# A hybrid decoder block on one core: a start-up branch taken out, a wider mask product, and a row finish moved into the next pass

## The chip, the core and the metric

One core of a Trainium2 chip runs one program, which holds the whole decoder block. TensorE (PE in the rows) multiplies; its weight loads (PEld) have rows of their own. VectorE (DVE), ScalarE (ACT) and GpSimd (POOL) work beside it, and SyncE (SP) mostly issues DMAs; ACT and POOL can issue DMAs too. Each engine works through its own list of instructions in order and waits on semaphores for the others. The metric is the device time of one execution in microseconds. Runs of a kernel spread by a few tenths of a per cent.

## What is computed

One layer over 1024 rows of width 1024, cut to what matters here:

```python
hn = rmsnorm(h, norm_mix_g);  proj = hn @ w_in            # split into the parts of both attentions and two gates
o_a = indexed_sparse_attention(a_q, a_k, a_v, i_q, i_k, i_w, positions, topk=256)
o_b = latent_attention(q_nope, q_rope, k_nope, k_rope, v_b, positions)
h = h + (sigmoid(g_a) * (o_a @ w_branch_a) + sigmoid(g_b) * (o_b @ w_branch_b)) @ w_out
u = causal_depthwise_conv(rmsnorm(h, norm_ffn_g) @ w_up);  gate, val = split(u)
h = h + (silu(gate) * val) @ w_down                       # 2816 -> 1024
return rmsnorm(h, norm_final_g)
```

Both attentions mask by position: a key counts where its position is not above that of the query. `setup_inputs` gives the positions 0 to 1023, so that the mask is the plain causal one; a kernel has to be right for any positions.

## The kernel before

**Arithmetic.** Every float32 operand is split into a rounded high part (`split`, line 150, on ACT for the most part) and the rest (line 156, a subtraction on DVE or POOL), and `mm3` (lines 180 to 182) multiplies high by high, high by low and low by high. All 128x512 products are of this kind.

**Two versions in one program.** `Block(..., True)` is written for rising positions and uses the triangle; `Block(..., False)` takes any. `emit` (line 1880 on) first loads the positions on SP and ACT, compares neighbours on DVE (lines 1902 to 1907), sums the flags over the partitions with a small PE product (line 1908), writes a flag (line 1909), and every engine loads it into a register and branches (`tc.If(rising > 0)`). The first block then runs; when it finds a choice of keys too close to call, it writes `redo` (line 837, DVE). At the end every engine loads `redo`, and branches over the second block.

**The start of the block.** `load_x` (line 530 on) sets a tile to zero, multiplies it 12 times to warm PE (line 233), and loads the first weights (line 486) and rows of x (line 544) on SP; DVE and POOL split the weights (lines 152 and 156), ACT and DVE scale and split x (lines 549 and 550). `prologue` builds constants (lines 451 to 464), the triangle `tri` and an identity in bfloat16 among them.

**The mask product.** `scores` (line 695 on) adds the triangle on PE: between the products of a diagonal tile (line 711) stands one product of the identity with `tri` (line 710), 128x128 in bfloat16, whose neighbours are float32 products of 256 to 512 columns. There are 80 in an execution.

**The end.** `ffn_down` goes through seven passes (`plan`, p = 0 to 6) of K = 11 steps, four row blocks (qb) to a step; three matmuls each make 132 in a pass. A step needs two operands, s and t: both are formed from loaded rows by subtractions on POOL (lines 1778 to 1785 in `down_prepare`) and then split, high part on ACT, low part on DVE. The loads of `down_fetch` (line 1724) go by SP and take tiles of one ring (`AS` of them), which the squares and scaled rows use as well. After the last step of a pass the results are added to the rows `H` on DVE (line 1799, `add`). Row blocks 0 to 3 are complete after p = 5, blocks 4 to 7 after p = 6. A complete block is squared and summed on ACT (line 1815), scaled by the gain on POOL (line 1821), and `finish` works out the reciprocal root on DVE: the two half sums are added (line 1827), and `rsqrt` (lines 163 to 174) makes three Newton steps of two small operations each. ACT (line 1834) or DVE (line 1836) then multiplies, and SP stores (line 1837). A scheduler sets the order on each engine when the program is built: it is static, and code that is written later tends to stand later.

## Time and profile before

| | us |
|---|---|
| median of three runs (lowest, highest) | 1614.48 (1614.17, 1618.14) |
| the profiled execution, own time | 1617.39 |
| its span in the trace | 1615.5 |
| PE busy | 1514.8 |
| DVE busy | 1210.2 |
| POOL busy | 918.4 |
| ACT busy | 783.0 |

PE is busy for 94% of the span. The places where it isn't are few, and two of them lie at the ends: ahead of the first product, and in and behind the last pass. A row of the timeline has the start, the duration, the engine and line, the operation with its operands, and in brackets how long the engine was idle before it and on whom it waited. A matmul's duration is longer than the distance to the next one, since they are pipelined; it is the distance of starts that counts.

### The profile page before, as it was taken

How to read it: one execution, taken by the hardware profiler on the slowest of the kernel's cores; microseconds unless marked ns; L12 is line 12 of the kernel's file. 1: busy time of each engine (PE TensorE's matmuls, PEld its weight loads, DVE VectorE, ACT ScalarE, POOL GpSimd, SP SyncE). 2: the span in 40 equal slices, each digit the busy share in tenths (PEclk: the TensorE clock that was granted, in tenths of full speed). 3: DMA queues.
4: the chain of work that ended last, by engine and by line, in shares of the span. 5: the costliest groups of instructions: out<-in, count | busy, mean ns of one | idle time of the engine just before them, and what ended most of it. 6: DMA issues, size and time to landing. Idle time of an engine off the chain costs nothing. (4 is left out here: it accounts for less than half of the span.)

```text
span 1615.5 us, 21528 instructions
## 1 busy us (share of the span) xinstructions
PE 1514.8 (94%) x7312; PEld 1248.7 (77%) x7312; DVE 1210.2 (75%) x1959; ACT 783.0 (48%) x1437; POOL 918.4 (57%) x758
## 2 busy tenths in 40 slices
PE   8979999989899999999999788999999999989985
PEld 7768888877677777898878677888888887768864
DVE  7268999934578887885635986878877776895996
ACT  3635522223367787775422544444444544434434
POOL 3141222511666767665622689888877773586773
PEclk9989999989999999999999899999999999999997
DMA  6321132420200023213752122222222205854333
GB/s 220 133 95 60 53 102 97 131 92 32 100 14 17 14 82 95 72 60 123 238 193 79 46 79 79 79 78 79 88 82 90 93 26 207 312 178 134 127 99 138
DMA packets 74841, 166.23 MB, mean 103 GB/s; under 512 B 9634, under 2 KB 14114, under 8 KB 74722
## 3 DMA queue, kind: packets, MB, share of 16 engines
q1 hardware_dynamic: 64496, 142.74, 26.7%
q10 hardware_dynamic: 7634, 13.64, 2.3%
q0 software_dynamic: 2592, 8.39, 1.3%
q8 instruction: 59, 0.97, 0.2%
q14 instruction: 60, 0.49, 0.1%
HBM read 123.94 MB, written 40.53 MB: 102 GB/s over the span
## 5 line engine op out<-in xcount | busy, mean ns | idle before, releaser
L182 PE MATMUL tc<-tc,tc 128*128 128x512 f32 (+2 forms) x1420 | 546.0, 385 | 7.5 <-POOL tc L156 5.6
L180 PE MATMUL tc<-tc,tc 128*128 128x512 f32 (+2 forms) x1420 | 542.3, 385 | 8.1 <-ACT tc L598 2.4
L181 PE MATMUL tc<-tc,tc 128*128 128x512 f32 (+2 forms) x1420 | 546.7, 385 | 1.2 <-POOL tc L156 1.0
L156 POOL TENSOR_TENSOR tc<-tc,tc 128x512 fp32r<-128x512 f32 (+2 forms) x182 | 300.8, 1659 | 246.0 <-ACT tc L150 229.4
L150 ACT ACTIVATE tc<-tc 128x512 fp32r<-128x512 f32 (+1 forms) x362 | 230.3, 659 | 350.0 <-PE tc L181 219.9
L180 PEld LDWEIGHTS tc<-tc,tc 128*128 128x128 f32 x1420 | 271.2, 191 | 63.8 <-ACT tc L598 2.8
L182 PEld LDWEIGHTS tc<-tc,tc 128*128 128x128 f32 x1420 | 271.2, 191 | 60.2 <-POOL tc L156 6.2
L181 PEld LDWEIGHTS tc<-tc,tc 128*128 128x128 f32 x1420 | 270.4, 190 | 54.0 <-POOL tc L156 1.3
L156 DVE TENSOR_TENSOR tc<-tc,tc 128x512 fp32r<-128x512 f32 x184 | 223.1, 1245 | 45.4 <-ACT tc L150 38.8
L181 PE MATMUL tc<-tc 128*128 128x512 f32 x332 | 133.5, 405 | 12.0 <-DVE tc L156 11.8
L1142 POOL TENSOR_SCALAR tc<-tc,tc 128x128 f32<-128x128 f32 (+7 forms) x128 | 95.1, 748 | 69.3 <-DVE tc L1141 55.8
L182 PE MATMUL tc<-tc 128*128 128x512 f32 x332 | 131.7, 400 | 0.4 <-DVE tc L156 0.4
L180 PE MATMUL tc<-tc 128*128 128x512 f32 x332 | 124.2, 399 | 3.8 <-ACT tc L150 3.5
L1140 ACT ACTIVATE tc<-tc,tc 128x128 f32<-128x128 f32 (+7 forms) x128 | 96.4, 753 | 33.0 <-DVE tc L1134 15.7
L1674 DVE SCALAR_TENSOR_TENSOR tc<-tc,tc,tc 128x1023 f32<-128x1023 f32 x44 | 65.1, 1482 | 53.7 <-ACT tc L1673 53.6
L711 PE MATMUL tc<-tc 128*128 128x384 f32 (+4 forms) x352 | 90.0, 370 | 8.4 <-DVE tc L644 5.7
L1675 DVE SCALAR_TENSOR_TENSOR tc<-tc,tc,tc 128x1022 f32<-128x1022 f32 x44 | 93.6, 2126 | 1.4
L181 PEld LDWEIGHTS tc<-tc 128*128 128x128 f32 x332 | 63.9, 192 | 31.2 <-DVE tc L156 18.6
L711 PE MATMUL tc<-tc,tc 128*128 128x512 f32 (+4 forms) x288 | 78.0, 386 | 8.6 <-ACT tc L1140 7.9
L180 PEld LDWEIGHTS tc<-tc 128*128 128x128 f32 x332 | 63.3, 192 | 18.9 <-ACT tc L150 5.4
L711 PEld LDWEIGHTS tc<-tc 128*128 128x128 f32 x352 | 61.5, 194 | 18.0 <-DVE tc L644 6.5
L182 PEld LDWEIGHTS tc<-tc 128*128 128x128 f32 x332 | 64.0, 193 | 14.6 <-DVE tc L156 1.5
(260 smaller groups left out, 2466.6 us busy)
## 6 DMA issues: line engine op xcount, KB each, us to landing
tc<-tc SPq DMA_DIRECT2D x144, 256.0 KB, 3.3
tc<-in_w_up SPq DMA_DIRECT2D x44, 512.0 KB, 3.7
tc<-in_w_down SPq DMA_DIRECT2D x77, 256.0 KB, 4.3
tc<-tc ACTq DMA_DIRECT2D x52, 256.0 KB, 2.0
tc<-tc SPq DMA_DIRECT2D x20, 512.0 KB, 2.6
tc<-in_w_g SPq DMA_DIRECT2D x16, 512.0 KB, 3.7
tc<-tc POOLq DMA_DIRECT2D x24, 256.0 KB, 2.4
tc<-in_w_c SPq DMA_DIRECT2D x10, 512.0 KB, 4.1
```

Source lines behind the costliest of these rows:

```text
L150: self.last_split = nc.scalar.activation(hi, src, AF.Copy)
L156: e.tensor_tensor(lo, src, hi.bitcast(F32), op=OP.subtract)
L180: x = [mm(ps, lhs[0], rhs[0], start=start, stop=False, **kw), mm(ps, lhs[0], rhs[1], start=False, stop=False, **kw), mm(ps, lhs[1], rhs[0] ...
L181: mm(ps, lhs[0], rhs[1], start=False, stop=False, **kw),
L182: mm(ps, lhs[1], rhs[0], start=False, stop=stop, **kw)]
L711: self.last_score = mm(ps[:, j * 512:j * 512 + n], l, r[:, o:o + n], start=i == 0, stop=i == len(lhs) - 1)
L1140: self.last_exp = nc.scalar.activation(p3, src, AF.Exp, bias=nm, scale=-1.0, accum_out=l)
L1142: nc.gpsimd.tensor_scalar(p, p, l, 0.0, op0=OP.mult, op1=OP.add)
L1674: v.scalar_tensor_tensor(o[:, 1:], x[:, :S - 1], cw[:, t, 1:2], o[:, 1:], op0=OP.mult, op1=OP.add)
L1675: v.scalar_tensor_tensor(o[:, 2:], x[:, :S - 2], cw[:, t, 0:1], o[:, 2:], op0=OP.mult, op1=OP.add)
```

## The change

The flag and its branch at the start are gone: the first block always runs. The comparison of neighbouring positions is kept, as `rising` at the end of `prologue`, on six small DVE operations with two loads on the ACT queue; it counts into `bad`, so that positions that don't rise set `redo`, and the second block then runs as before.

The mask product takes the type of its neighbours and is 256 columns wide: `tri` is a triangle between two blocks of zeros, of which the needed 256 columns are cut out, and the identity is a copy of the same type.

The row finish is written anew. `partial` works out the half that is known early (POOL, after p = 1 and p = 4). `finish` takes a square root on ACT, a reciprocal on DVE and one Newton step, four DVE operations instead of eleven, and its stores go on the ACT queue where ACT multiplied. For blocks 0 to 3, the adds, squares, scaling and finish are no longer written at the end of p = 5: `close` is called after the steps k = 1 to 4 of p = 6, a block a step.

```diff
-            self.tri = self.t(c, [P, P], BF16)
-            v.tensor_scalar(self.tri, jp, 0.0, BIG, op0=OP.is_gt, op1=OP.mult)
-            self.ident_b = self.t(c, [P, P], BF16)
-            v.tensor_copy(self.ident_b, self.ident)
+            self.tri = self.t(c, [P, 3 * P], F32R)
+            v.tensor_scalar(self.tri[:, :P], jp, 0.0, None, op0=OP.mult)
+            v.tensor_scalar(self.tri[:, P:2 * P], jp, 0.0, BIG, op0=OP.is_gt, op1=OP.mult)
+            v.tensor_scalar(self.tri[:, 2 * P:], jp, 0.0, None, op0=OP.mult)
+            self.ident_r = self.t(c, [P, P], F32R)
+            v.tensor_copy(self.ident_r, self.ident)
...
+            self.rising()
...
-                    e = j * 512 + (n if W == cw else W)
-                    mm(ps[:, e - P:e], self.ident_b, self.tri, start=False, stop=False, skip_group_check=True)
+                    e = j * 512 + n
+                    mm(ps[:, e - 256:e], self.ident_r, self.tri[:, P if W < cw else 0:][:, :256], start=False, stop=False,
+                       skip_group_check=True)
...
+    def rising(self):
+        nc, v = self.nc, self.nc.vector
+        pr = self.a["pos_r"]
+        pi, kh, kl = [self.kd[:, o:o + 9].bitcast(I32) for o in (768, 784, 800)]
+        d1, d2 = [self.kd[:, o:o + 8] for o in (816, 832)]
+        nc.scalar.dma_start(pi[:P - 1], bass.AP(tensor=pr.tensor, offset=pr.offset, ap=[[8, P - 1], [1, 9]]))
+        nc.scalar.dma_start(pi[P - 1:], pr[:, S - 9:])
...
+        v.tensor_scalar(d1, d1, 0.0, 0.0, op0=OP.is_le, op1=OP.add, accum_out=self.bad[:, 0:1])
...
+        def partial(b):
+            e = int(b >= 4)
+            x = self.t(dn, [P, 2], F32, tag="ss4", bufs=8)
+            g.tensor_scalar(x[:, 0:1], squares[b][:, e:e + 1], 1.0 / D, EPS, op0=OP.mult, op1=OP.add)
+            g.tensor_scalar(x[:, 1:2], x[:, 0:1], -0.5, 0.0, op0=OP.mult, op1=OP.add)
+            known[b] = x
         def finish(b):
-            v.tensor_add(ss, s2[:, 0:1], s2[:, 1:2])
-            v.tensor_scalar(ss, ss, 1.0 / D, EPS, op0=OP.mult, op1=OP.add)
-            self.rsqrt(c, r, ss, 1)
+            e = int(b < 4)
+            s, x = squares[b][:, e:e + 1], known[b]
+            r, t, y = [self.t(dn, [P, 1], F32, tag=k, bufs=3) for k in ("r3", "t3", "y3")]
+            nc.scalar.activation(r, s, AF.Sqrt, scale=1.0 / D, bias=x[:, 0:1])
+            v.scalar_tensor_tensor(t, s, -0.5 / D, x[:, 1:2], op0=OP.mult, op1=OP.add)
+            v.reciprocal(r, r)
+            v.scalar_tensor_tensor(t, r, t, r, op0=OP.mult, op1=OP.mult)
+            v.scalar_tensor_tensor(y, t, 1.5, r, op0=OP.add, op1=OP.mult)
             for hf in (1, 0):
...
-                nc.sync.dma_start(self.out[b * P:(b + 1) * P, cs], x)
+                (nc.scalar if by_act else nc.sync).dma_start(self.out[b * P:(b + 1) * P, cs], x)
...
+                if late and k >= LATE:
+                    close(*late.pop(0))
             for qb in range(4):
...
                 for rh, hf in plan[p][2]:
+                    if p == 5:
+                        late.append((p, rh, hf, qb))
+                    else:
+                        close(p, rh, hf, qb)
...
-    with tc.If(rising > 0):
-        Block(tc, a, out, True, {"redo": redo}).run()
+    Block(tc, a, out, True, {"redo": redo}).run()
```

`close` holds what stood in the loop before (add, square, scale, finish, and `partial` where the early half is squared).

**On DVE, where p = 5 goes over into p = 6.** Before, the two low pieces of step k = 4 (rows 1737 and 1741; L156, line 156) stand between the Newton operations (lines 163 to 174) of four blocks:

```order
1730 L1827 TENSOR_TENSOR tc_13915<-tc_12875 128x1
1731 L170 SCALAR_TENSOR_TENSOR tc_13839<-tc_13835,tc_13842 128x1
1732 L1828 TENSOR_SCALAR tc_13888<-tc_13888 128x1
1733 L170 SCALAR_TENSOR_TENSOR tc_13866<-tc_13862,tc_13869 128x1
1734 L1828 TENSOR_SCALAR tc_13915<-tc_13915 128x1
1735 L174 SCALAR_TENSOR_TENSOR tc_13835<-tc_13839,tc_13835 128x1
1736 L163 TENSOR_SCALAR tc_13892<-tc_13888 128x1
1737 L156 TENSOR_TENSOR tc_3245<-tc_12267,tc_3245 128x512
1738 L174 SCALAR_TENSOR_TENSOR tc_13862<-tc_13866,tc_13862 128x1
1739 L163 TENSOR_SCALAR tc_13919<-tc_13915 128x1
1740 L170 SCALAR_TENSOR_TENSOR tc_13839<-tc_13835,tc_13842 128x1
1741 L156 TENSOR_TENSOR tc_3245<-tc_13808,tc_3245 128x512
```

Now, in the same place, with the lines of the changed kernel (157 is the old 156; 1859 to 1862 are the new `finish`; rows 1717 and 1719 are step k = 3, rows 1724 and 1727 step k = 4):

```order
1717 L157 TENSOR_TENSOR tc_3210<-tc_12231,tc_3210 128x512
1718 L1859 SCALAR_TENSOR_TENSOR tc_13862<-tc_12828,tc_12830 128x1
1719 L157 TENSOR_TENSOR tc_3210<-tc_13778,tc_3210 128x512
1720 L1859 SCALAR_TENSOR_TENSOR tc_13900<-tc_12835,tc_12837 128x1
1721 L1860 RECIPROCAL tc_13861<-tc_13861 128x1
1722 L1860 RECIPROCAL tc_13899<-tc_13899 128x1
1723 L1861 SCALAR_TENSOR_TENSOR tc_13862<-tc_13861,tc_13862 128x1
1724 L157 TENSOR_TENSOR tc_3210<-tc_12232,tc_3210 128x512
1725 L1861 SCALAR_TENSOR_TENSOR tc_13900<-tc_13899,tc_13900 128x1
1726 L1862 SCALAR_TENSOR_TENSOR tc_13863<-tc_13862,tc_13861 128x1
1727 L157 TENSOR_TENSOR tc_3210<-tc_13797,tc_3210 128x512
1728 L1862 SCALAR_TENSOR_TENSOR tc_13901<-tc_13900,tc_13899 128x1
```

Between the four adds and the second low piece of k = 4 stand 24 operations before and 10 now.

**On POOL, at the same place.** Before, the eight gain products of blocks 0 to 3 (line 1821) stand in one piece between the subtractions (line 1785) of k = 4 and k = 5:

```order
722 L1785 TENSOR_TENSOR tc_13808<-tc_13808,tc_12278 128x512
723 L1821 TENSOR_TENSOR tc_13830<-tc_12345,tc_12353 128x512
724 L1821 TENSOR_TENSOR tc_13832<-tc_12345,tc_12353 128x512
725 L1821 TENSOR_TENSOR tc_13857<-tc_12346,tc_12353 128x512
726 L1821 TENSOR_TENSOR tc_13859<-tc_12346,tc_12353 128x512
727 L1821 TENSOR_TENSOR tc_13884<-tc_12347,tc_12353 128x512
728 L1821 TENSOR_TENSOR tc_13886<-tc_12347,tc_12353 128x512
729 L1821 TENSOR_TENSOR tc_13911<-tc_12348,tc_12353 128x512
730 L1821 TENSOR_TENSOR tc_13913<-tc_12348,tc_12353 128x512
731 L1785 TENSOR_TENSOR tc_13935<-tc_13935,tc_12279 128x512
```

Now (1807 is the old 1785, 1843 the old 1821; the first row is k = 6):

```order
738 L1807 TENSOR_TENSOR tc_13835<-tc_13835,tc_12245 128x512
739 L1843 TENSOR_TENSOR tc_13857<-tc_12310,tc_12318 128x512
740 L1843 TENSOR_TENSOR tc_13859<-tc_12310,tc_12318 128x512
741 L1843 TENSOR_TENSOR tc_13895<-tc_12311,tc_12318 128x512
742 L1843 TENSOR_TENSOR tc_13897<-tc_12311,tc_12318 128x512
743 L1807 TENSOR_TENSOR tc_13873<-tc_13873,tc_12246 128x512
744 L1807 TENSOR_TENSOR tc_13911<-tc_13911,tc_12247 128x512
745 L1843 TENSOR_TENSOR tc_13933<-tc_12312,tc_12318 128x512
746 L1843 TENSOR_TENSOR tc_13935<-tc_12312,tc_12318 128x512
747 L1843 TENSOR_TENSOR tc_13971<-tc_12313,tc_12318 128x512
748 L1843 TENSOR_TENSOR tc_13973<-tc_12313,tc_12318 128x512
749 L1807 TENSOR_TENSOR tc_13949<-tc_13949,tc_12248 128x512
```

The subtractions of k = 5 and 6 now stand ahead of the gain products, those of k = 7 and 8 between them, those of k = 9 and 10 behind them.

**On ACT, at the end.** Before, the four squares (line 1815) come first and then the four last products (line 1834):

```order
1290 L1815 ACTIVATE tc_14121,tc_13587<-tc_12350 128x512
1291 L1815 ACTIVATE tc_14158,tc_13594<-tc_12351 128x512
1292 L1815 ACTIVATE tc_14195,tc_13601<-tc_12352 128x512
1293 L1834 ACTIVATE tc_13582<-tc_13582,tc_14089 128x512
1294 L1834 ACTIVATE tc_13589<-tc_13589,tc_14126 128x512
1295 L1834 ACTIVATE tc_13596<-tc_13596,tc_14163 128x512
1296 L1834 ACTIVATE tc_13603<-tc_13603,tc_14200 128x512
```

Now (1837 is the square, 1858 the root, 1868 the product, 1871 a store):

```order
1306 L1868 ACTIVATE tc_13562<-tc_13562,tc_14047 128x512
1307 L1868 ACTIVATE tc_13572<-tc_13572,tc_14076 128x512
1308 L1871 DMA out_dram<-tc_13562 128x512
1309 L1871 DMA out_dram<-tc_13572 128x512
1310 L1868 ACTIVATE tc_13582<-tc_13582,tc_14105 128x512
1311 L1837 ACTIVATE tc_14128,tc_13587<-tc_12317 128x512
1312 L1871 DMA out_dram<-tc_13582 128x512
1313 L1858 ACTIVATE tc_14132<-tc_13587,tc_13589 128x1
1314 L1868 ACTIVATE tc_13592<-tc_13592,tc_14134 128x512
1315 L1871 DMA out_dram<-tc_13592 128x512
```

The product of block 6 (row 1310) now stands ahead of the square of block 7 (row 1311), and ACT issues four of the last eight stores.

## Rows read from the trace of the kernel before

**Rows 1.** The table of stretches: start and end of the stretch, its length, then for PE, PEld, DVE, ACT and POOL the busy time with the number of instructions, the granted PE clock, the DMA share and GB/s.

```profile
11.00:30.00 19.00, 19.00 (x85) 16.08 (x84) 17.76 (x24) 8.92 (x9) 9.28 (x5) 1.00 0.81 282
1560.00:1580.00 20.00, 13.96 (x56) 10.61 (x54) 18.60 (x52) 9.04 (x20) 12.25 (x9) 0.89 0.26 82
1580.00:1600.00 20.00, 18.76 (x72) 15.03 (x72) 14.63 (x27) 9.07 (x18) 9.73 (x7) 0.86 0.31 103
```

**Rows 2.** The timeline of the first 11.6 us: the flag (lines 1889 to 1909), the block's first load, and what leads to the first product.

```profile
0.73 0.36 SPq L1889 DMA_DIRECT2D pi<-in_pos_r  x1
...
1.30 1.28 ACT L1901 ACT_TABLE_LOAD   x1 [1.30 <-PEq L1967]
...
3.18 0.17 DVE L1902 TENSOR_SCALAR kh<-pi 128x9 int32<-128x9 int32 x1 [2.30 <-DMA pi<-in_pos_r]
...
4.42 0.15 DVE L1909 TENSOR_SCALAR fl<-ps 1x1 int32<-1x1 f32 x1 [0.28 <-PE ps L1908]
5.22 0.36 SPq L486 DMA_DIRECT2D tc<-in_w_c  x1
...
6.75 0.25 DVE L458 TENSOR_SCALAR tc<-tc 128x128 f32<-128x128 f32 x1
...
9.02 0.67 DVE L152 CAST tc<-tc 128x976 fp32r<-128x976 f32 x1 [2.02 <-DMA tc<-in_w_c]
...
11.28 0.61 PE L180 MATMUL tc<-tc,tc 128*128 128x488 f32 x1
```

**Rows 3.** The timeline of PE around two mask products (line 710), and four products of 256 columns in a row a little later.

```profile
418.88 0.28 PE L711 MATMUL tc<-tc,tc 128*128 128x256 f32 x1
419.00 0.23 PE L710 MATMUL tc<-tc,tc 128*128 128x128 bf16 x1
419.04 0.36 PE L711 MATMUL tc<-tc,tc 128*128 128x256 f32 x1
419.24 0.23 PE L710 MATMUL tc<-tc,tc 128*128 128x128 bf16 x1
...
421.88 0.63 PE L711 MATMUL tc<-tc,tc 128*128 128x256 f32 x4
```

**Rows 4.** Groups of instructions by line and shape, of the whole span: the mask product, and the weight loads of it and of its neighbours. Behind the bar: busy us and mean ns of one.

```profile
L710 PE MATMUL tc<-tc,tc 128*128 128x128 bf16 x80 | 18.9, 236 | 0.0
...
L711 PEld LDWEIGHTS tc<-tc,tc 128*128 128x128 f32 x288 | 50.0, 202 | 15.3 <-ACT tc L1140 11.6 <-POOL tc L1142 1.1
L710 PEld LDWEIGHTS <-tc 128*128 128x128 bf16 x80 | 7.9, 99 | 10.6 <-issue 7.5
```

**Rows 5.** The timelines of DVE and PE from the end of p = 4 into p = 5.

```profile
1533.09 24.47 DVE L156 TENSOR_TENSOR tc<-tc,tc 128x512 fp32r<-128x512 f32 x17
...
1536.39 0.50 PE L181 MATMUL tc<-tc 128*128 128x512 f32 x1 [1.55 <-DVE tc L156]
```

**Rows 6.** The timeline of PE in p = 6: its start, the two waits, and the last products.

```profile
1560.18 0.39 PE L180 MATMUL tc<-tc 128*128 128x512 f32 x1
...
1569.70 0.39 PE L180 MATMUL tc<-tc 128*128 128x512 f32 x1
1574.00 0.50 PE L181 MATMUL tc<-tc 128*128 128x512 f32 x1 [3.91 <-DVE tc L156]
...
1581.11 2.08 PE L180 MATMUL tc<-tc 128*128 128x512 f32 x4 [3.25 <-ACT tc L150]
...
1597.67 0.39 PE L180 MATMUL tc<-tc 128*128 128x512 f32 x1
...
1599.48 0.39 PE L182 MATMUL tc<-tc 128*128 128x512 f32 x1
```

**Rows 7.** The timelines of DVE, POOL and ACT in the same stretch.

```profile
1564.33 1.25 DVE L1827 TENSOR_TENSOR tc<-tc 128x1 f32<-128x1 f32 x1
1565.51 0.68 DVE L156 TENSOR_TENSOR tc<-tc,tc 128x512 fp32r<-128x512 f32 x1
...
1573.26 0.68 DVE L156 TENSOR_TENSOR tc<-tc,tc 128x512 fp32r<-128x512 f32 x1
...
1561.30 9.75 POOL L1821 TENSOR_TENSOR tc<-tc,tc 128x512 f32<-128x512 f32 x7 [4.30 <-issue]
...
1583.27 6.39 POOL L1785 TENSOR_TENSOR tc<-tc,tc 128x512 f32<-128x512 f32 x4 [5.27 <-DMA tc<-in_w_down]
...
1575.22 2.56 ACT L1834 ACTIVATE tc<-tc,tc 128x512 f32<-128x512 f32 x4 [9.37 <-issue]
```

**Rows 8.** The timelines behind the last product: the last add, the last square, ACT's last products, SP's last eight stores.

```profile
1601.28 0.69 DVE L1799 TENSOR_TENSOR tc<-tc,tc 128x512 f32<-128x512 f32 x1
...
1602.00 0.63 ACT L1815 ACTIVATE tc<-tc 128x512 f32<-128x512 f32 x1 [2.62 <-DVE tc L1799]
...
1602.05 1.27 POOL L1821 TENSOR_TENSOR tc<-tc,tc 128x512 f32<-128x512 f32 x1 [1.60 <-DVE tc L1799]
...
1603.95 4.81 SPq L1837 DMA_DIRECT2D out_dram<-tc  x8
...
1606.14 1.37 ACT L1834 ACTIVATE tc<-tc,tc 128x512 f32<-128x512 f32 x2 [1.40 <-DVE tc L174]
```

**Rows 9.** The timelines of DVE and SP where `redo` is written.

```profile
379.66 0.14 DVE L837 TENSOR_SCALAR redo<-tc 1x1 int32<-1x1 f32 x1
...
405.92 5.57 SPq L978 DMA_DIRECT2D tc<-tc  x2
```

## What I expected, and why

> **What bounds the kernel now.** I read the busy shares first: PE works 94% of the span, so a gain has to come from the few places where PE has nothing to do. The table of stretches then says where the change can reach. From 11 to 30 us PE is full [rows 1], so what counts at the start is when the first product comes, at 11.28 [rows 2]. From 1560 to 1580 PE is busy 13.96 of 20 us, and up to 1600 its clock is granted at 0.86 to 0.89 [rows 1]: that is p = 6. The timeline of PE shows p = 6 beginning at 1560.18 and its last product at 1599.48 [rows 6]. Its 132 matmuls at 0.226 (eight steps in 1.81, rows 1597.67 to 1599.48) would take 29.9 us; they take 39.5. [...] Behind the last product 16 us remain to the span's end.
>
> **The start.** The block's first load is issued at 5.22; the flag's own first load went out at 0.73 [rows 2]. Without the flag the load takes its place: 5.22 - 0.73 = **4.5 us** earlier, and all that hangs on it, the first product among it. What is added lies beside it. ACT issues two position loads and then loads its table (1.28), which the flag's wait hid; the first scaling of x on ACT waits for the weight cast anyway (at 9.02, so about 4.5 in the new count), and by then the queue is long done. DVE gets two more constants at 0.25, where it waited 2.02 for the weights, and six operations like that of 0.17 while it is busy 17.76 of 19 us [rows 1, 2]. The six overlap to about 1 us, as they did in the flag (3.18 to 4.14); bounds are nothing and 1.4 us lost. I take nothing, since PE was full with DVE at that load.
>
> SP must load `redo` into a register, and now does so early in its list. In the trace `redo` is written at 379.66 and SP's next transfer goes at 405.92 [rows 9]: 26 us of cover. Were that cover gone, SP would hold back everything by as much as the write is late.
>
> **The mask product.** Starts tell the cost: 419.00 for the mask, 0.04 to the next product, whose follower comes 0.20 later instead of 0.12 [rows 3]. So 0.12 of it is the mask's (0.04 plus 0.08). A 256-column product of the neighbours' type takes (0.63 - 0.27) / 3 = 0.12 [rows 3], with 0.27 the duration of one. 80 of them: no change, bounds plus or minus 80 x 0.05 = 4 us at the most. What speaks against it is the weight load: 99 ns for the mask in bfloat16, 202 for its neighbours [rows 4]. The four products at 0.12 had weight loads of the long kind and were not held up by them.
>
> [...]
>
> **From p = 4 to p = 6.** DVE subtractions and POOL products slow each other: 17 low pieces take 24.47 us here, 1.44 each [rows 5], where one alone takes 0.68; and an addition of one column takes 1.25 beside POOL [rows 7], which is a POOL product (9.75 / 7 = 1.39). So, beside a busy POOL, a DVE operation on two SBUF operands costs about one POOL product, and a low piece right behind such a small one comes for 0.68 more. I count by that. Before, the second low piece of k = 4 had 24 operations ahead of it and ended at 1573.94, with PE wanting it at 1569.93. Now 10 are ahead, 8 of them with two operands. POOL is kept busy from 1560 (the subtractions of k = 5 and 6 now come earlier, four gain products, then k = 7 and 8, then block 2). Eight operations in five slots (small ones in pairs or with a low piece) to nine slots of 1.39 to 1.53 from 1562.9 give 1570.5 to 1576; I take the lower third, 1571.5, so that this wait is about 2 instead of 4.1. Next, ACT holds the high piece of k = 5 behind four products by 1/rms (2.56 [rows 7]), as before; they wait for the last small operation of block 1, right behind k = 4. So k = 5 comes about 0.6 + 0.7 + 2.6 after k = 4, and PE has 12 x 0.226 = 2.7 us of k = 4 to do: a wait of 1 to 2 us remains of 3.4. Then k = 9 and 10 stand on POOL behind all eight gain products, and their loads wait for stores of blocks 0 and 1; by the same slots they come about 1 to 2 us late. That they are wanted only near 1582 and 1585 is what keeps it small. [...]
>
> Against that, p = 4 into p = 5: eight tiny POOL operations wait for ACT's squares between the gain products and delay the first subtraction of p = 5 by some 0.8 us; DVE has no gap there for 24 us and PE has already waited 1.55 [rows 5], so this goes through: 0.8 to 2 lost, I take 1.2. Sum **2.3 us** gained, bounds 9.6 gained and 3 lost.
>
> ACT also loads its table once for the root, 1.28 by the row [rows 2]; it stands behind block 1's square and ahead of work that has some 2 us. [...]
>
> **The end.** Before, the last add comes at 1601.28, 1.8 behind the last product, held by Newton steps; ACT ends at 1607.51 and SP, with eight stores in a row, at 1608.76, 9.3 behind [rows 6, 8]. Now, from the last product: add at 2.1 (two DVE products and the roots of blocks 4 and 5 ahead of it), 0.69; the gain product 1.27, behind which DVE's last operation of block 6 waits (0.14); ACT's product of block 6 (0.72) and only then the square of block 7 (0.63 + 0.19); root 0.3, reciprocal and two small operations 0.45, product 0.72, store 0.45. Sum 7.7, against 9.3: **1.6 us** saved, with the stores shared by two queues. SP's flag load at the end falls away, ACT's remains; no row shows either, so I keep 0 to 1 for the range.
>
> **Sum.** 4.5 + 0 + 2.3 + 1.6 = 8.4 us. The profiled execution would go from 1617.39 to 1609.0; it lies 2.9 above the median of the runs, so the median goes from 1614.48 to **1606.1**. Elsewhere the scheduler has swapped neighbours, around the start of the sparse attention above all; I give that 2 us either way.
>
> **The rivals.** *p = 6 runs through.* If a small DVE operation doesn't cost a POOL product when the blocks come one by one, k = 4 is in time and with it the rest: 9.6 instead of 3.5, minus 1.2, and 1614.5 - 4.5 - 8.4 - 1.6 = 1600.0. For it: the two operations that took 1.25 and 0.68 in one slot [rows 7]. Against it: POOL has the same fourteen products to make in the same pass.
> *p = 6 gains nothing.* If each small operation takes a slot, k = 4 comes at 1576, PE waits 6 there, and only the second wait shrinks: 1608.4 with no gain, 1611 at the bound of 3 lost.
> *The weight load counts.* If 80 loads show their 0.1 us more, 8 us go: 1614. [...]
> *The start isn't regained.* If the first loads are as late as the first instructions of a program allow (the flag's load landed 2.3 us after its issue, nothing shows what the code costs), 1610.5.
> *Slower.* One mechanism: the wide mask product runs at a quarter of its neighbours' rate, 0.48 instead of 0.12. 80 x 0.36 = 29 us, less 8.4: 1635. It decides from 0.12 + (8.4 + 4.8) / 80 = 0.29 us each. Against it: products of the same width and type at 0.12.
>
> **How the numbers follow.** The forecast (1603 to 1609) gets 0.50, p = 6 running through 0.16, no gain in p = 6 0.20, the weight load 0.06, the start 0.05, slower 0.03. A measurement tells 0.3% from no change, 4.8 us: below 1609.6 is faster. The first two, and the better part of the third (0.12), are faster: 0.78. The rest of the third, the load and the start are the same: 0.19. Slower 0.03. The range takes in the second case and the whole third: 1599.5 to 1611, leaving out some 0.14.
>
> **What would show it.** Right: the first load at about 0.7 and the first product at 6.8; starts 0.12 before and after a mask product; in p = 6 a first wait near 2 us with DVE as releaser and a second, smaller one with ACT; ACT's last store 7 to 8 us behind the last product. Wrong: a PE wait in p = 5 above 3 us, `LDWEIGHTS` ahead of a mask wait, a stretch outside these that moves by more than 2 us, or SP idle near 380 us with loads behind it.

## The result, and the profile after

The changed kernel takes **1606.77 us** (median of 12 runs, 1600.10 to 1610.88), against 1616.51 of the kernel before on the same chip (12 runs, 1611.44 to 1622.23): a ratio of 0.9938, with a 95% interval of 0.9921 to 0.9955. The profiled execution takes 1604.8 us, its span is 1603.0; before these were 1617.39 and 1615.5.

To see where the 12.5 us between the two spans come from, the traces are cut at marks that both have. Each trace holds 7218 matmuls from the first product of the block on, the mask's not counted, so the n-th product of one answers to the n-th of the other. *Start* is where the 193rd product begins (the first of the second stage; it waits for ACT), *middle* goes from there to the first of the last 264 products (p = 5 and p = 6), *passes* to the last product, *tail* to the span's end.

| profiled execution | start | middle | passes | tail | span |
|---|---|---|---|---|---|
| before | 56.8 | 1469.3 | 73.4 | 16.0 | 1615.5 |
| after | 52.9 | 1463.8 | 72.0 | 14.3 | 1603.0 |
| gained | 3.9 | 5.5 | 1.4 | 1.7 | 12.5 |

**The start.** SP and ACT on the timeline of the kernel after, against [rows 2]:

```profile
0.73 0.40 SPq L491 DMA_DIRECT2D tc<-in_w_c  x1
1.18 0.54 ACTq L841 DMA_DIRECT2D tc<-in_pos_r  x1
1.18 1.36 SPq L549 DMA_DIRECT2D tc<-in_xT  x3
1.74 2.32 ACTq L842 DMA_DIRECT2D tc<-in_pos_r  x1
...
5.95 1.28 ACT L554 ACT_TABLE_LOAD   x1 [5.95 <-DMA tc<-in_xT]
7.24 2.38 ACT L554 ACTIVATE tc<-tc,tc 128x512 fp32r<-128x512 f32 x3
...
8.02 1.38 PE L181 MATMUL tc<-tc,tc 128*128 128x488 f32 x5 [1.08 <-ACT tc L554]
8.76 0.33 SPq L412 DMA_DIRECT2D tc<-in_pos_t  x1
...
9.13 0.43 SPq L549 DMA_DIRECT2D tc<-in_xT  x1
```

The first load goes out at 0.73, 4.49 earlier than 5.22. But the first product comes at 8.02, only 3.26 earlier than 11.28, and the next piece of x is issued at 9.13, 1.04 earlier than before (10.17). What SP waited for in between, from the table of waits (total us, times, longest):

```profile
SPq L412 <- DMA tc<-in_pos_r: 2.5, 1, 2.5
SPq L403 <- DMA tc<-in_norm_mix_g: 1.7, 1, 1.7
```

The longer wait is for the position loads of `rising`, issued on ACT's queue at 1.18 and 1.74: SP's load of `pos_t` stands behind their landing, and the loads of x behind that. The other is for the gain of the first rmsnorm, which also comes on ACT's queue.

The end of the stage, first before and then after (ACT squares rows of x, then copies the first projection; PE waits for that copy):

```profile
53.92 1.06 ACT L556 ACTIVATE tc<-tc 128x1024 f32<-128x1024 f32 x1 [1.47 <-DMA tc<-in_x]
55.13 1.06 ACT L556 ACTIVATE tc<-tc 128x1024 f32<-128x1024 f32 x1
56.18 1.02 ACT L598 ACTIVATE tc<-tc 128x488 f32<-128x488 f32 x2
56.79 0.79 PE L180 MATMUL tc<-tc,tc 128*128 128x512 f32 x1 [2.40 <-ACT tc L598]
```

```profile
48.23 1.06 ACT L561 ACTIVATE tc<-tc 128x1024 f32<-128x1024 f32 x1 [2.23 <-DMA tc<-in_x]
51.27 1.04 ACT L561 ACTIVATE tc<-tc 128x1024 f32<-128x1024 f32 x1
52.31 1.02 ACT L603 ACTIVATE tc<-tc 128x488 f32<-128x488 f32 x2
52.92 0.50 PE L181 MATMUL tc<-tc,tc 128*128 128x512 f32 x1 [2.09 <-ACT tc L603]
```

PE has nothing to do for 2.1 to 2.4 us here, in both. What ends the stage is therefore the chain of loads of x and ACT's squares, and not PE's first product.

**The middle.** The table of stretches, columns as in [rows 1]; the first two are of the kernel before, the others of the one after:

```profile
460.00:470.00 10.00, 8.01 (x43) 6.35 (x41) 7.80 (x19) 6.40 (x17) 9.66 (x12) 0.83 0.01 2
500.00:510.00 10.00, 7.99 (x41) 6.25 (x40) 9.06 (x19) 6.67 (x17) 9.65 (x11) 0.85 0.09 27
```

```profile
460.00:470.00 10.00, 9.71 (x63) 8.41 (x63) 8.26 (x19) 6.80 (x16) 5.94 (x10) 1.00 0.00 0
495.00:505.00 10.00, 7.99 (x55) 6.96 (x54) 8.51 (x20) 6.81 (x17) 9.66 (x11) 1.00 0.07 25
```

Before, the granted clock of PE falls in both places, to 0.53 from 466 to 468 us and to 0.50 from 508 to 510; after, it stays at 1.00, though PE stands still as long ahead of them (1.67 and 1.68 before, 1.70 and 1.68 after, each time for DVE). The first place is worth 1.6 us: the wait for DVE ends at 464.52 before and 459.80 after, 4.72 apart, and the next one at 474.76 and 468.40, 6.36 apart. Over the second, the distance of like products goes from 6.4 to 8.0. There is a third place, named in the expectations as 612 us: from 600 to 620 us the granted clock is 0.91 before and 1.00 after, and between 594 and 665 us the distance goes from 7.6 to 9.7.

**The mask product**, on the timeline of PE after, against [rows 3] (L716 is the mask, L718 its neighbours): starts 0.12 apart, as wide products are.

```profile
414.15 0.28 PE L718 MATMUL tc<-tc,tc 128*128 128x256 f32 x1
414.27 0.28 PE L716 MATMUL tc<-tc,tc 128*128 128x256 f32 x1
414.39 0.28 PE L718 MATMUL tc<-tc,tc 128*128 128x256 f32 x1
```

The weight load of the mask product now takes 192 ns, where [rows 4] have 99 for it and 202 for its neighbours; from the groups of instructions (busy us, mean ns, idle us before them):

```profile
L716 PEld LDWEIGHTS tc<-tc,tc 128*128 128x128 f32 x80 | 15.4, 192 | 0.6
```

**The passes**, PE after, against [rows 5, 6]: the first of six waits in p = 5, one more at the first step of p = 6 (which begins at 1550.95), and the others of p = 6.

```profile
1531.32 0.50 PE L183 MATMUL tc<-tc 128*128 128x512 f32 x1 [0.42 <-DVE tc L157]
...
1551.72 0.50 PE L182 MATMUL tc<-tc 128*128 128x512 f32 x1 [0.38 <-DVE tc L157]
...
1564.57 0.50 PE L182 MATMUL tc<-tc 128*128 128x512 f32 x1 [1.64 <-DVE tc L157]
...
1567.67 0.49 PE L181 MATMUL tc<-tc 128*128 128x512 f32 x1 [0.30 <-ACT tc L151]
1568.47 0.50 PE L182 MATMUL tc<-tc 128*128 128x512 f32 x1 [0.31 <-DVE tc L157]
...
1575.65 0.50 PE L182 MATMUL tc<-tc 128*128 128x512 f32 x1 [1.45 <-DVE tc L157]
1576.91 0.72 PE L181 MATMUL tc<-tc 128*128 128x512 f32 x2 [0.52 <-ACT tc L151]
```

The big waits of [rows 6] are gone. From its first product to its last p = 6 takes 37.7 us, and 40.7 before, where it begins at 1558.82: the 1560.18 from which the prediction counts is its seventh product. So it now loses 8.0, where 11.0 were lost. Counted from start to start, less the 0.23 of a product, 0.5 of it is at k = 0, 1.8 at k = 4, 1.0 at k = 5, 2.3 at k = 9 and 10, and 1.5 behind these, where the granted clock is 0.59 (1577 to 1580 us) and 0.77 (1580 to 1582); the rest is spread thinly. The pass p = 5 takes 34.3, and 32.8 before: six waits lose 3.5, where two lost 2.3. POOL shows why they are there: the new half of the finish (L1849, L1850) stands between its products.

```profile
1519.71 0.51 POOL L1849 TENSOR_SCALAR tc<-tc 128x1 f32<-128x1 f32 x1
...
1529.26 0.19 POOL L1850 TENSOR_SCALAR tc<-tc 128x1 f32<-128x1 f32 x1
1529.41 8.11 POOL L1804 TENSOR_TENSOR tc<-tc,tc 128x512 f32<-128x512 f32 x5
```

**The end**, against [rows 8]: the timelines behind the last product, which starts at 1588.66.

```profile
1590.72 0.67 DVE L1821 TENSOR_TENSOR tc<-tc,tc 128x512 f32<-128x512 f32 x1
...
1591.53 1.26 POOL L1843 TENSOR_TENSOR tc<-tc,tc 128x512 f32<-128x512 f32 x1 [1.87 <-DVE tc L1861]
1591.55 1.25 DVE L1862 SCALAR_TENSOR_TENSOR tc<-tc,tc 128x1 f32<-128x1 f32 x1
1592.84 0.72 ACT L1868 ACTIVATE tc<-tc,tc 128x512 f32<-128x512 f32 x1 [1.72 <-DVE tc L1862]
...
1593.47 0.61 ACT L1837 ACTIVATE tc<-tc 128x512 f32<-128x512 f32 x1
...
1595.18 0.72 ACT L1868 ACTIVATE tc<-tc,tc 128x512 f32<-128x512 f32 x1 [0.68 <-DVE tc L1862]
...
1595.93 0.34 ACTq L1871 DMA_DIRECT2D out_dram<-tc  x1
```

Add at 2.06 behind the last product, the small DVE operation beside POOL's product (1.25), then ACT's product, the last square, the last product and the store, which ends at 1596.27, 7.61 behind.

### The profile page after: what moved, and what is told of

It is laid out like the page before. It is cut to its first block, busy times and chain, and to the rows that moved or that the text cites. A ratio compares the mean times of both kernels' runs of the same rounds, so it can differ in the third digit from the quotient of the medians.

```text
span 1603.0 us, 21473 instructions
## 1 busy us (share of the span) xinstructions
PE 1508.8 (94%) x7310; PEld 1250.2 (78%) x7310; DVE 1207.1 (75%) x1902; ACT 785.7 (49%) x1445; POOL 928.5 (58%) x774
## 4 chain that ended last, share of the span: by engine, by line
PE 61%; DVE 20%; issue 6%; POOL 5%; ACT 4%; DMA 3%; SPq 0%; ACTq 0%; DVEq 0%; POOLq 0%
PE tc L182 16%; PE tc L183 16%; PE tc L181 16%; PE tc L718 6%; DVE tc L793 2%; POOL tc L157 2%; DMA tc<-tc 2%; DVE tc L157 2%; PE tc L1223 2%; PE tc L1370 2%; PE tc L1355 2%; PE tc L1204 1%; DVE tc L742 1%; POOL tc L1791 1%; DVE tc L997 1%
## 5 line engine op out<-in xcount | busy, mean ns | idle before, releaser
L157 DVE TENSOR_TENSOR tc<-tc,tc 128x512 fp32r<-128x512 f32 x184 | 219.8, 1229 | 46.4 <-ACT tc L151 40.0
L1162 ACT ACTIVATE tc<-tc,tc 128x128 f32<-128x128 f32 (+7 forms) x128 | 96.5, 754 | 32.3 <-DVE tc L1156 13.5
L718 PE MATMUL tc<-tc 128*128 128x384 f32 (+4 forms) x352 | 89.5, 365 | 10.2 <-DVE tc L649 6.6
L182 PEld LDWEIGHTS tc<-tc 128*128 128x128 f32 x332 | 63.2, 190 | 30.1 <-DVE tc L157 15.9
L718 PE MATMUL tc<-tc,tc 128*128 128x512 f32 (+4 forms) x288 | 75.6, 362 | 9.1 <-ACT tc L1162 8.4
L718 PEld LDWEIGHTS tc<-tc 128*128 128x128 f32 x352 | 60.5, 191 | 19.9 <-DVE tc L649 7.5
L183 PEld LDWEIGHTS tc<-tc 128*128 128x128 f32 x332 | 63.6, 192 | 14.6 <-DVE tc L157 2.0
```

The lines of the kernel that those rows point to most:

```text
L157: e.tensor_tensor(lo, src, hi.bitcast(F32), op=OP.subtract)
L182: mm(ps, lhs[0], rhs[1], start=False, stop=False, **kw),
L183: mm(ps, lhs[1], rhs[0], start=False, stop=stop, **kw)]
L718: self.last_score = mm(ps[:, j * 512:j * 512 + n], l, r[:, o:o + n], start=i == 0, stop=i == len(lhs) - 1)
L1162: self.last_exp = nc.scalar.activation(p3, src, AF.Exp, bias=nm, scale=-1.0, accum_out=l)
```

## The experiments

**Theory A**: the parts add up as predicted; the start falls short because of the position loads (and of ACT's table load, which now shows), and the middle is chance of the clock. **Theory B**: the middle comes from the mask product's type. The kernels below are built from the kernel before (first four) or the changed one (the others). Where an expectation speaks of the gain at 25 to 50 us, it was read from like rows set side by side; the mark of the 193rd product, counted, is used here in its place. Where one says that p = 6 gains 4.3 and p = 5 loses 2.9, it counts p = 6 from its seventh product; from the first it is 3.0 and 1.5.

| run | median (runs) | before beside it | ratio, 95% interval | start | middle | passes | tail |
|---|---|---|---|---|---|---|---|
| e1, before again | 1614.60 (11) | 1614.69 | 1.0000, 0.9988 to 1.0012 | 56.6 | 1470.1 | 72.8 | 16.1 |
| e2, mask alone | 1613.91 (12) | 1614.69 | 0.9996, 0.9982 to 1.0009 | 56.2 | 1466.0 | 73.5 | 16.3 |
| e3, start alone | 1608.37 (12) | 1614.69 | 0.9963, 0.9950 to 0.9977 | 54.4 | 1465.6 | 71.3 | 15.0 |
| e4, finish alone | 1612.96 (12) | 1614.69 | 0.9992, 0.9974 to 1.0010 | 56.3 | 1466.0 | 70.6 | 14.2 |
| e5, after again | 1606.37 (6) | 1614.54 | 0.9948, 0.9930 to 0.9966 | 55.0 | 1462.4 | 72.1 | 14.2 |
| e6, early table | 1613.05 (12) | 1614.54 | 0.9981, 0.9964 to 0.9999 | 54.2 | 1472.4 | 71.7 | 14.1 |
| e7, half on ACT | 1602.98 (7) | 1614.54 | 0.9938, 0.9915 to 0.9961 | 54.9 | 1464.1 | 71.4 | 13.5 |
| e8, not late | 1606.89 (6) | 1614.54 | 0.9953, 0.9936 to 0.9971 | 53.0 | 1463.4 | 71.2 | 15.9 |
| e9, late positions | 1602.85 (6) | 1613.00 | 0.9946, 0.9932 to 0.9961 | 52.8 | 1460.6 | 72.0 | 14.6 |
| e10, pad | 1613.32 (12) | 1613.00 | 0.9999, 0.9988 to 1.0010 | 55.2 | 1472.1 | 71.7 | 14.2 |
| e11, three edits | 1602.94 (6) | 1613.00 | 0.9935, 0.9918 to 0.9952 | 52.2 | 1463.7 | 71.2 | 13.5 |
| e12, two edits | 1603.59 (6) | 1614.75 | 0.9930, 0.9912 to 0.9949 | 52.8 | 1465.9 | 71.4 | 13.5 |

### e1: the kernel before, unchanged

> The kernel before, unchanged. Theory A (the 4.9 us that the changed kernel gained between 465 and 660 us are stretches at the lower PE clock that come and go between executions of one kernel): ratio 1.000 within 0.002, and the list of low-clock stretches in the trace differs from that of the first execution of before, the ones at 466, 507 and 612 us among those that may be gone. Theory B (the bfloat16 mask product brings these stretches): they are there again, at the same places within 1 us.

The low clock came back in the same places (460 to 470: 0.83, 500 to 510: 0.87), in a second profiled execution:

```profile
460.00:470.00 10.00, 8.00 (x44) 6.34 (x43) 7.88 (x18) 6.64 (x17) 9.73 (x12) 0.83 0.03 9
500.00:510.00 10.00, 8.00 (x43) 6.36 (x41) 9.05 (x19) 6.71 (x16) 9.65 (x11) 0.87 0.08 27
```

This profiled execution took 1617.46, 2.9 above its median, as that of before did.

### e2, e3, e4: one part alone

e2 takes the mask of the diff ahead, e3 the start (no flag, `rising` in `prologue`), e4 the finish (`partial`, `finish`, `close` and `late`); each leaves the rest as before.

```diff
 # e2
+            self.tri = self.t(c, [P, 3 * P], F32R)
+                    mm(ps[:, e - 256:e], self.ident_r, self.tri[:, P if W < cw else 0:][:, :256], ...
 # e3
-    with tc.If(rising > 0):
-        Block(tc, a, out, True, {"redo": redo}).run()
+    Block(tc, a, out, True, {"redo": redo}).run()
 # e4
+                if late and k >= LATE:
+                    close(*late.pop(0))
```

> The mask product of the change alone. Theory A: ratio 1.000 within 0.002 (a gain of 0 to 1 us at most, 0.12 us for either form of the product). Theory B (the mask product in the type of its neighbours keeps the clock up): ratio 0.997, 4 to 5 us less, and no low-clock stretch at 466, 507 and 612 us. Theory C (the longer weight load counts): 1.005.

> The start of the change alone. Both theories: 4.5 us less, ratio 0.9972, with the first product 3.3 us earlier (the table load of ACT stands behind a wait for x) and the rest of the 4.5 caught up by 110 us. If the start were not what brings it: 3.3 us or less from there on, 0.998.

> The row finish of the change alone (partial, finish, close one step later). From the two traces: p = 5 loses 2.9, p = 6 gains 4.3, the end behind the last product gains 1.7, so 3 us less, ratio 0.998. Rival (p = 5 lost its 2.9 us for another reason, such as the order that came with the other parts): p = 5 as before and 6 us less, ratio 0.9963.

The mask alone changes nothing that can be told. The start alone gains 0.37% (1614.69 x 0.0037 = 6.0 us, 3.7 to 8.1), of which its trace shows 2.1 to 2.4 by the start's mark. The finish alone gains 0.08%, 1.3 us, with an interval that takes in none and 4.2; its trace shows 2.3 to 2.9 in the passes and 1.8 to 1.9 in the tail. In the passes p = 6 gains 3.9 to 4.5, and p = 5, at 34.4, loses 1.6 as in the changed kernel. One profile's passes also vary with nothing changed in them: e3 has the old finish in the old order, and its passes, at 71.3, are 1.5 to 2.1 shorter than those of e1 (72.8) and before (73.4).

The low clock at 460 to 470 and 500 to 510 is missing from all three (1.00 each), and e3 and e4 still have the narrow mask. Theory B falls: the mask doesn't decide it. e4 says more: until far beyond these places it is the kernel before, the same instructions in the same order on the same tiles, and its middle is 3.3 to 4.1 shorter all the same. So the instructions up to there don't decide it either. What is left is chance of an execution, or something in the program that their order doesn't show; two profiles with it and twelve without don't tell these apart. The place at 612 us is another matter: from 600 to 620 us the granted clock is 0.91 in before and e1 to e4, and 1.00 in the changed kernel.

### e5: the changed kernel, unchanged

> The changed kernel, unchanged. Ratio to before 0.994 within 0.002; in the trace the gains over before by place are to be the same within 0.5 us where the order of work makes them (first product 3.3 us earlier, p = 5 loses 2.9, p = 6 gains 4.3, the end 1.7), while low-clock stretches may differ. If a gain by place is gone here, it was of the one execution.

Middle, passes and tail agree with the first profile within 1.4 us. The start doesn't: its mark is at 55.03, 2.1 later, with the same program.

### e6 and e10: ACT's table early, and a pad

```diff
 # e6; e10 has the first two lines alone
+        one = self.t(c, [P, 1])
+        nc.vector.memset(one, 1.0)
+        nc.scalar.activation(one, one, AF.Copy)
         z = self.view(0, [512])
```

> The changed kernel with one added ACT operation on a constant ahead of the block's work, so that ACT loads its table at about 2 us and not behind its wait for x. If the table load is what took 1.2 us of the expected 4.5: first product at about 6.8 instead of 8.0, and 1.2 us less than the changed kernel from there on (ratio to before 0.993). Rival: another wait takes its place (the weight cast, or DVE's low pieces of x) and the first product comes earlier without anything behind 50 us.

> The changed kernel with one more tile of 128x1 in the pool of constants, set once and never read, and nothing else: 4 bytes in each partition move the tiles behind it. If that is what cost the kernel with the early table load its 9 us between 1000 and 1350 us: PE makes some 430 products of 512 columns in 100 us there instead of 438, and the time is 1613 (ratio 0.998 to before). If the cost came from the early table load itself: 438 in 100 us, and 1606.5.

In e6 the table's 1.28 is hidden and the first product comes at 7.10 in place of 8.02. PE is then 4.4 ahead of before at its 101st product (29.45 against 33.83). At the stage's end it is 2.6 ahead, and the changed kernel in its two profiles 3.9 and 1.8; PE waits there:

```profile
54.15 0.69 PE L181 MATMUL tc<-tc,tc 128*128 128x512 f32 x1 [4.30 <-ACT tc L606]
```

So the earlier first product isn't what sets the stage's end. But the kernel was slower than the changed one by 0.3%, and its middle longer by 8.6. e10, which has the tile and its memset and no ACT work, is as long there. Between 1100 and 1200 us, where PE never waits and its clock is 1.00, PE makes 430 products in e10 and 438 in the changed kernel (the second row):

```profile
1100.00:1200.00 100.00, 100.00 (x430) 80.36 (x429) 75.81 (x57) 47.86 (x66) 79.08 (x48) 1.00 0.22 79
```

```profile
1100.00:1200.00 100.00, 100.00 (x438) 82.05 (x437) 79.95 (x58) 48.65 (x68) 81.16 (x48) 1.00 0.22 79
```

In the built programs the new tile takes 32 bytes of each partition, and not the 4 that the expectation of e10 has. The tiles placed behind it in the same part of SBUF stand 32 bytes on, others where they stood. e11 (below) has e6's memset and its operation on ACT, but in a tile that was there already: its tiles stand as in the changed kernel, and it makes 438. So what e6 lost was the place of tiles, and not ACT's work, and its time says nothing of the table load.

### e7: the early half on ACT

```diff
-            g.tensor_scalar(x[:, 0:1], squares[b][:, e:e + 1], 1.0 / D, EPS, op0=OP.mult, op1=OP.add)
-            g.tensor_scalar(x[:, 1:2], x[:, 0:1], -0.5, 0.0, op0=OP.mult, op1=OP.add)
+            nc.scalar.activation(x[:, 0:1], squares[b][:, e:e + 1], AF.Copy, scale=1.0 / D, bias=EPS)
+            nc.scalar.activation(x[:, 1:2], x[:, 0:1], AF.Copy, scale=-0.5)
```

> The changed kernel with the two small operations of partial on ACT instead of POOL. If they are what p = 5 loses its 2.9 us to: PE's waits on DVE in p = 5 (0.4 to 0.6 in most steps) go, p = 5 gets 2 to 3 us back, ratio to before about 0.9925. Rival (POOL makes the subtractions of k = 5 and 6 of p = 6 already in p = 5, without a pause in which DVE could catch up): p = 5 still loses 2 us or more.

Without the eight tiny operations PE's waits in p = 5 shrink from six to three, which lose 2.8, 0.5 more than before the change:

```profile
1529.39 0.50 PE L182 MATMUL tc<-tc 128*128 128x512 f32 x1 [1.58 <-DVE tc L157]
1532.80 0.50 PE L182 MATMUL tc<-tc 128*128 128x512 f32 x1 [0.62 <-DVE tc L157]
1536.22 0.50 PE L183 MATMUL tc<-tc 128*128 128x512 f32 x1 [0.17 <-DVE tc L157]
```

The pass p = 5 takes 33.2, against 34.3 with them, so these operations cost it 1.1 (they take POOL itself 3.4). A new wait of 0.6 at k = 3 of p = 6 takes part of this back. The median, at 1602.98, is 3.4 below that of e5 on the same chip, though the intervals overlap.

### e8: the rows finished at the end of p = 5, as before, with the new finish

```diff
-                    if p == 5:
-                        late.append((p, rh, hf, qb))
-                    else:
-                        close(p, rh, hf, qb)
+                    close(p, rh, hf, qb)
```

> The changed kernel with blocks 0 to 3 closed at the end of p = 5, as before, but with the new finish. If it is the later place that p = 6 gains by: p = 6 gains less than 2 of its 4.3 us, and the ratio to before is 0.996. If it is the shorter finish (four DVE operations for eleven): p = 6 as in the changed kernel within 1 us.

The time is that of the changed kernel. Its passes are 0.8 to 0.9 shorter and its tail 1.6 to 1.7 longer. In p = 6 PE waits 2.88 at k = 4, in place of 1.64, and 1.9 at k = 5, and no longer at k = 9 and 10:

```profile
1564.91 0.50 PE L182 MATMUL tc<-tc 128*128 128x512 f32 x1 [2.88 <-DVE tc L157]
```

The shorter finish alone takes the 3.91 of [rows 6] down to this. The later place isn't what shortens p = 6. Nor is it shown to shorten the tail: the last store of e8 ends 7.71 behind its last product, 7.61 in the changed kernel, so the finish is as quick.

```profile
1595.02 0.34 ACTq L1871 DMA_DIRECT2D out_dram<-tc  x1
```

The longer tail lies behind that store, 8.2 us against 6.7 to the span's end; its cause isn't shown.

### e9 and e12: the positions loaded behind x

```diff
-            self.rising()
...
-                nc.scalar.activation(hi, st[:, cs], AF.Copy, scale=g)
+                last = nc.scalar.activation(hi, st[:, cs], AF.Copy, scale=g)
+        if self.causal:
+            with self.tc.issue_after(last.ins):
+                self.rising()
```

e12 has e7's edit too.

> The changed kernel with the comparison of positions, its two loads on the ACT queue among them, written behind the last piece of x instead of into the prologue. If SP's wait of 2.5 us for the position load (and with it the later pieces of x behind it) is what kept the start from bringing 4.5 us: that wait is gone, the third piece of x is issued at 6 to 7 us instead of 9.1, and the gain over before is 4 us or more from 25 to 50 us on, where the changed kernel has 2.7; ratio to before 0.9935. Rival (the x pieces wait for DVE's low pieces and for their tiles anyway): SP's wait changes its releaser, and the gain at 25 to 50 us stays below 3.2.

> Two edits of the changed kernel together, without the early table load: the positions are loaded behind the last piece of x, and the early half of the row finish stands on ACT. What decides the start is where PE waits for ACT's copy of the first projection, its 193rd product of the first stage. In four profiles with the flag it starts at 56.16 to 56.79, in seven with the positions loaded at the start at 52.92 to 55.23 (mean 54.2), in two with late positions at 52.19 and 52.81. Theory A (the position loads on ACT's queue hold SP's loads of x, and these hold the squares of x on ACT ahead of that copy): at 52 to 53 again, so 4 gained on the kernel before instead of 2.2. Rival (the spread among profiles is chance, and where the positions are loaded makes no difference): anywhere from 52.9 to 55.2, most likely above 53.0. Pass 5 loses 2.8 to 2.9 instead of 4.0, as with the half on ACT alone. Time: 1.8 for the start and 1.2 for pass 5 less than the changed kernel, a ratio to the kernel before of 0.993; by the rival 0.994 to 0.995.

SP no longer waits for positions. In e9 the next piece of x goes out at 5.37 instead of 9.13, and ACT's queue pays later: ACT stands idle for 2.93 while the second load is issued. Behind that it still waits for rows of x (1.4 and 2.0).

```profile
5.37 0.43 SPq L548 DMA_DIRECT2D tc<-in_xT  x1
...
33.25 3.84 ACTq L844 DMA_DIRECT2D tc<-in_pos_r  x1
37.20 1.06 ACT L563 ACTIVATE tc<-tc 128x1024 f32<-128x1024 f32 x1 [2.93 <-issue]
...
52.81 0.50 PE L181 MATMUL tc<-tc,tc 128*128 128x512 f32 x1 [2.89 <-ACT tc L605]
```

Now all profiles can be set side by side by the start's mark. With the flag (before, e1, e2, e4): 56.2 to 56.8, mean 56.5. With the positions at the start (after, e3, e5, e6, e7, e8, e10): 52.9 to 55.2, mean 54.2. With late positions (e9, e11, e12): 52.2, 52.8, 52.8, mean 52.6. The change as made gains 2.2 on the mean at this mark; with late positions it is 3.9. In medians, e9 alone can't be told from the changed kernel (0.9946 against 0.9938 and 0.9948).

### e11: late positions, half on ACT, table early, with no tile moved

```diff
+        one = self.kd[:, 900:901]
+        nc.vector.memset(one, 1.0)
+        nc.scalar.activation(one, one, AF.Copy)
```

> The changed kernel with three edits: positions compared behind the last piece of x, partial on ACT, and the early table load on a column of a tile that is there already, so that no tile moves. If each counts: first product at 7.1, start 4 us or more, p = 5 loses 1.2 us less, and no slow stretch from 1000 to 1350: 1602 to 1603.5, ratio 0.9925. If low-clock stretches or new waits eat it: 1605 or more.

Hiding the table's 1.28 gives no more at the start than chance would (52.2 against 52.8 twice), though the first product comes at 6.04. It came out no faster than e7, e9 or e12: ratios of 0.9930 to 0.9946, whose intervals overlap. In e11 and e12 PE waits 4.4 us for DVE at 322 us where it waits 2.3 in e9 and in the changed kernel; this eats what the start gave, and its cause was not looked into. In e10 PE waits 4.5 there too, some 2 of what its middle lost. Each of e7, e9, e11 and e12 is faster than the kernel before; that one of them beats the changed kernel isn't shown.

## Why the prediction was right, and where it wasn't

The time (1606.77 for 1606.1) came out right, with two terms too large and one stage that gave what wasn't forecast. In the profiled execution 1609.0 was predicted and 1604.8 measured. That the total comes so close is in part luck: start, passes and end together gave 7.0 of the 8.4 predicted in the profile compared, and 5.3 with the mean of seven for the start; the middle, put at nothing, made up for it. By medians the three parts alone gain 0.37%, 0.04% and 0.08%, together 0.49%, where the whole change gains 0.52% (e5) to 0.62%.

- **The start, 4.5 predicted.** Mis-sized: 3.9 in the profile compared, 2.2 on the mean of seven. Two steps failed. From PE being full from 11 to 30 us the prediction concludes "what counts at the start is when the first product comes": what counts is the copy that PE waits for at 56.79, behind loads and squares of x; in e6 the first product comes 4.2 earlier than before and the one behind this copy 2.6. And the two position loads were costed at nothing beside ACT's wait, where SP was the engine held: 2.5 in the table of waits. Moving them gave 1.6 back on the mean of three profiles. The first load at 0.73 came as predicted, the first product 1.2 later than the 6.8 given.
- **The mask, 0 predicted.** Right: 0.12 each, and 0.9996 alone in e2. The longer weight load is there (192 ns for 99) and PE doesn't wait for it (starts 0.12 apart). The rivals of the weight load and of the quarter rate are out.
- **p = 4 to p = 6, 2.3 predicted.** Mechanism right, size 1.4 (against 73.1, the mean of the two profiles of before: 1.1, and 1.0 in e5). p = 6 gained 3.0 for 3.5: k = 4 waits 1.8 ("about 2"), k = 5 waits 1.0 (the low end of 1 to 2), k = 9 and 10 wait 2.3 (1 to 2). The 2.3 is 3.5 for p = 6 less 1.2 for p = 5, and the 3.5 has 1 us in it for one wait less with the lower clock behind it; no run shows that term by itself. What the profiles show is a granted clock of 0.89 from 1560 to 1580 us and 0.86 from 1580 to 1600 before [rows 1], and in p = 6 of the changed kernel of 1.00 up to 1575, 0.75 from there to 1580 and 0.95 to its end. p = 5 lost 1.5 for 1.2, and e7 shows that 1.1 of it is the tiny POOL operations. That the later place was part of the gain, as the slots assumed, doesn't hold: e8. With 1.5 to 2.1 of chance in e3's passes, one profile can't tell 1.4 from 2.3. Over all profiles the four with the old finish have passes of 72.7 on the mean and the ten with the new one 71.5: 1.2.
- **The table for the root.** It is loaded in p = 6 for 1.28 (an ACT row of the kernel after), and the root starts right behind it:

```profile
1556.58 1.28 ACT L1858 ACT_TABLE_LOAD   x1
1557.88 0.48 ACT L1858 ACTIVATE tc<-tc,tc 128x1 f32<-128x1 f32 x2
```

  Nothing else stands beside it: 0.02 lies between the two rows, and the load starts 0.01 behind the end of the operation ahead of it on ACT.
- **The end, 1.6 predicted.** Right step by step up to the last store (add at 2.06 for 2.1, store ending at 7.61 for 7.7). What follows that store was left as it was, and it was: 6.8 before, 6.7 after. That is in part luck: with the same finish it is 8.2 in e8 and 5.9 in e7, e11 and e12, so the tail's 1.7 could as well have been 0.1 or 2.5.
- **The middle, 0 with 2 either way.** Wrong in the profile: 5.5 gained, which by the prediction's own list is a sign against it. Some 3 us of it are two places at 464 and 507 where the granted clock falls (0.83 and 0.85 over 10 us, 0.83 and 0.87 in e1) in both profiles of the kernel before and in none of an altered one. The mask isn't the cause (e3, e4), and neither are the instructions up to there (e4, which has the same). Some 2 more go with the place at 612 us. Both profiled executions of before lie 2.9 above the median of their program, and their mean granted clock, 0.971, is at the low end of its runs, of which most stand at 0.973 and above; the first two places make 0.002 of it. That would fit if most executions were without these two, but none of those was traced, so what the middle gives in the medians stays open. e3's trace gains 2.4 at the start, 3.7 in the middle, 2.1 in the passes and 1.0 in the tail; which of them make the 6.0 of its median isn't shown.

## What to carry to other kernels

The first product was no measure of the start here (4.2 earlier in e6, and 2.6 left where PE waits for ACT): look for the first wait that PE can't avoid, and follow that chain back to the queue that feeds it. A load that is added on another queue can still hold the queue that matters, through a wait that the scheduler sets behind it: two on ACT's queue held SP for 2.5 us here. Eight tiny operations on POOL, whose products feed a full chain, cost PE 1.1 us; and one small tile that nothing reads made the middle of e10 8 to 10 us longer, so compare a kernel with a pad of the same size before you blame the work that it holds. A stretch that the change doesn't touch differed by 3 to 4 us with the same instructions in it (the middle of e4 against before and e1), so one profile of each kernel doesn't price a change of a few us.

## What the runs showed of the hardware

- **Thirty-two bytes of SBUF.** With one 128x1 tile more, and the tiles placed behind it in the same part of SBUF 32 bytes on, the pitch of back-to-back 512-column products goes from 100/438 = 0.228 us to 100/430 = 0.233, at a granted clock of 1.00 and with no wait of PE. From the 4801st product to the 6401st it is 374.1 us in e6 and e10 and 367.5 to 367.6 in the other twelve profiles, 6.5 apart. The whole middle is 8 to 10 us longer (e10 against the two profiles of the changed kernel), some 2 of it by the longer wait for DVE at 322 us. Which operands are hit wasn't tried.
- **A low clock behind a stop, or none behind the same stop.** At 464 and 507 us a stop of PE of 1.7 us for DVE is followed by products at a lower granted clock (0.83 to 0.87 over 10 us, 0.50 from 508 to 510 in the profile of before) in both profiles of the kernel before, and by none in any altered kernel (1.00). e4 is among these, with the same instructions up to there and a stop as long (1.68 at 463.77).
